# The last swiglu of a two-block diffusion transformer: products before the norm, operand parts side by side, all k tiles in one PSUM group

## The chip, the core and the metric

One core of a Trainium2 chip runs the whole kernel in one launch. The metric is the device time of that launch in microseconds: the median of several runs, and beside it one execution recorded by the hardware profiler, whose page and trace are read here. TensorE is called PE below, VectorE DVE, ScalarE ACT, GpSimd POOL and SyncE SP.

## What is computed

A block updates a latent sequence (256 tokens, 1024 features) and, where it is still read later, a context sequence of the same size: a gated swiglu, a mixer (short convolution in block 0, grouped attention in block 1) and a second gated swiglu. The part that the change rewrites is the end of block 1, for the 256 latent tokens alone: the output projection of the attention, the norm with its modulation, and the last swiglu.

```python
def _rms(t, g):
    y = t * lax.rsqrt(jnp.mean(t * t, axis=-1, keepdims=True) + NORM_EPS)
    return y * g

def _modulate(t, g, shift, scale):
    return _rms(t, g) * (1 + scale) + shift

def _swiglu(h, w13, w2):                       # w13: 1024 x 5632, w2: 2816 x 1024
    gte, up = jnp.split(h @ w13, 2, axis=-1)
    return (jax.nn.silu(gte) * up) @ w2

mod = (jax.nn.silu(c) @ mod_w[i] + mod_b[i])   # nine vectors of 1024 per block
...
lat = lat + mod[:, 1, 2] * (attention @ w_o)
lat = lat + 0.5 * mod[:, 2, 2] * _swiglu(
    _modulate(lat, norm_g[i, 2], mod[:, 2, 0], mod[:, 2, 1]), ffn_w13[i, 1], ffn_w2[i, 1])
```

Inputs, weights and result are 32-bit floats.

## The kernel before

**Layout.** Features lie on the 128 partitions, in `KT` = 8 tiles, and tokens on the free axis. The tile `x` holds 512 columns: latent tokens first (`S` = 256), then context (`T2` = 512 together). In the last part only the first 256 are computed.

**Products in three parts.** A product of two 32-bit operands is made from split operands. `split` (lines 97 to 99) writes `hi`, a rounded copy (ACT, line 98), and `lo`, the rest (DVE, line 99). `mm3` (lines 119 to 124) then issues three matmuls into one PSUM group: wh by mh, wh by ml, wl by mh. One call of `mm3` for one 128 x 128 weight tile is called a step. Weights come as raw tiles of up to 2048 columns over SP's queue (`load_raw`, tag `wr`, three buffers) and are split into halves of 1024 columns (`half`, tags `wh` and `wl`, four buffers each).

**The last swiglu.** `ffn(1, 1, hn, S, ...)` takes the hidden 2816 features as `NM` = 22 tiles, in `THIRDS` of 8, 7 and 7. For each tile `w13_mm` computes the gate half (`pg`) and the up half (`pu`), 8 k tiles each, 48 matmuls of 256 columns together; this is called a pair. `w13_post` applies silu (ACT), multiplies (DVE) and splits the product into `gh` and `gl`. After each third `project` multiplies the third's tiles by their part of w2, for 8 output tiles m (`py`), and `finish` adds the gated result to `x` (line 446, DVE). The last third's `finish` also sends each output tile from SP.

**The boundary before it.** The output projection is `project(by_pairs("wo"), ..., S, 0, 1)`. Its `tail_norm` squares each new tile of x and sums up over m (`square_add`, lines 220 to 228). After the last m, `rms_inv` sums over partitions on PE (line 237), takes the root (ACT), the reciprocal (DVE, line 246) and broadcasts the result with four small matmuls (line 248). `norm_k` then makes the normed, modulated operand parts `hh` and `hl` for each k (lines 256, 266 and 267), and the first pair's matmuls read them. `ready` (line 460) loads ACT's table for the root ahead of time.

**The modulation.** The nine vectors of each block are computed on DVE in 224 units (`mod_unit`, line 142, a product of 128 x 1024 with a row sum), from weight tiles that share the `wr` buffers and SP's queue with the others. They are spread over the kernel: `tick(n)` adds n to what is owed and issues that many whole units; `mod_ready` forces those that a vector still lacks when it is read. The argument `ev` of `ffn` and `project` is the number owed for each output tile m (1.7 in the second swiglu, 1.6 in the third). Four units belong to each 1 MB tile, but only two from vector 5 of block 1 on, where the context isn't needed any more.

**Order.** But for the opening, a scheduler of the framework lists the instructions of each engine ahead of time: among those that it reckons ready, the one written first. On the chip each engine goes through its list in order. PSUM is given out in eight banks, six of them (`psm`) for products, so three pairs can be open at once. `hot` hands out 1024 column tiles from a pool of 16, `gp` pairs of 512 column tiles, eight of each tag.

Of the kernel before, what the change touches and what calls it, by code (L numbers as in the profile page):

```python
# [9 lines left out]
F32 = mybir.dt.float32  # L10
F32R = mybir.dt.float32r
BF16 = mybir.dt.bfloat16
AF = mybir.ActivationFunctionType
ALU = mybir.AluOpType
AX = mybir.AxisListType

P = 128
D = 1024
KT = D // P
S = 256  # L20
T2 = 2 * S
NM = 22
# [19 lines left out]
def hybrid_kernel(ctx: ExitStack, tc: tile.TileContext, a: dict, out: bass.AP):  # L42
    nc = tc.nc
    const = ctx.enter_context(tc.tile_pool(name="const", bufs=1))
# [3 lines left out]
    gp = ctx.enter_context(tc.tile_pool(name="gp", bufs=8))  # L48
    tp = ctx.enter_context(tc.tile_pool(name="tp", bufs=2))
# [23 lines left out]
    x = act.tile([P, KT, T2], F32, name="x", tag="x")  # L73
# [140 lines left out]
    accs = {}  # L214
# [181 lines left out]
    def tail_norm(l, j, h):  # L396

        box = {}

        def tail(m, c0, c1):  # L400
            square_add(m, c0, c1)
            if m == KT - 1:
                if not box:
                    box["A"] = scale_of(l, j)
                    box["B"] = mod_ready(l, 3 * j)
                s = c0 // S

                def inv():
                    return rms_inv(s, (accs[s], accs[s, "last"]))

                def rest(part, ri):

                    if isinstance(h, Blocks):
                        h.block(s, part, box["A"], box["B"], ri, fine=s == 0 and part == 0)
                    else:
                        for k in range(4 * part, 4 * part + 4):
                            norm_k(s, k, h, box["A"], box["B"], ri)

                def both_parts():
                    ri = inv()  # L420
                    for part in range(2):
                        rest(part, ri)

                if s == 0:
                    keep = []

                    def one():
                        keep.append(inv())
                        rest(0, keep[0])

                    pending.append(one)
                    pending.append(lambda: rest(1, keep[0]))
                    if (l, j) == (1, 2):
                        flush()
                else:
                    flush()
                    pending.append(both_parts)

        return tail
# [268 lines left out]
    def lazy_gate(l, j):  # L708
        box = []

        def get():
            if not box:
                box.append(gate_of(l, j))
            return box[0]

        return get


    h = Plain()
# [11 lines left out]
    ris = []  # L731
    for s in range(2):
# [6 lines left out]
        out=sb1, in0=modb[:, 0, KT : 2 * KT], scalar1=1.0, scalar2=None, op0=ALU.add  # L739
# [81 lines left out]
    h = FirstBlocks(h, h32)  # L821
# [11 lines left out]
    hn = Plain()  # L833
    ffn(0, 0, h, T2, lazy_gate(0, 0), tail_norm(0, 1, hn), gs0)
    h = hn

    zs = []
    for m in range(KT):
# [16 lines left out]
        u = tp.tile([P, T2], F32, name=nm("u"), tag="gm", bufs=3)  # L855
# [21 lines left out]
    def by_pairs(key):  # L877
        box = {}

        def ws(m):  # L880
            if m // 2 not in box:
                box[m // 2] = load_w(a[key][m // 2])
            w = box[m // 2]
            return lambda k: w(k * 256 + (m % 2) * P)

        return ws

    hn = Blocks()
# [3 lines left out]
    )  # L892
    h = hn
    hn = Blocks()
    ffn(0, 1, h, T2, lazy_gate(0, 2), tail_norm(1, 0, hn), (), 1.7)
    h = hn


    hn = Plain()
    ffn(1, 0, h, T2, lazy_gate(1, 0), tail_norm(1, 1, hn), (), 1.6)  # L900
    h = hn
    ap = ctx.enter_context(tc.tile_pool(name="ap", bufs=2))

# [192 lines left out]
    for hd in range(HEADS):  # L1096
# [6 lines left out]
    mix(HEADS - 1, pts.pop(HEADS - 1))  # L1103


    hn = Plain(S)
    project(
        by_pairs("wo"), lambda k, c0, c1: aos[k], KT, lazy_gate(1, 1), tail_norm(1, 2, hn), S, 0, 1,
    )
    ffn(  # L1110
        1, 1, hn, S, lazy_gate(1, 2),
        lambda m, c0, c1: nc.sync.dma_start(out[m], x[:, m, :S]),
    )


def _layout(inp):
    f = lambda k: np.asarray(inp[k])
    d = {}

    def kp(w, width):  # L1120

        k, n = w.shape
        v = w.reshape(k // P, P, n // width, width).transpose(2, 1, 0, 3)
        return v.reshape(n // width, P, (k // P) * width)

    tok = np.concatenate([f("x")[0], f("ctx")[0]], axis=0)
    d["xT"] = tok.T.reshape(KT, P, T2).transpose(1, 0, 2)
    d["c2"] = np.stack([f("c")[0], f("c_ctx")], axis=0)
    d["ccol"] = d["c2"].reshape(2, KT, P).transpose(2, 1, 0)
    mw = f("mod_w")  # L1130
    m0 = mw[0][:, : 2 * D].reshape(KT, P, 2, 4, S)
    d["mod0"] = m0.transpose(2, 3, 1, 0, 4).reshape(2, 4, P, 2048)
    d["modT"] = mw.transpose(0, 2, 1).reshape(2, 36, 2, P, D).transpose(0, 1, 3, 2, 4).reshape(2, 36, P, 2048)
    d["modb"] = f("mod_b").reshape(2, 72, P).transpose(2, 0, 1)
    d["normg"] = f("norm_g").reshape(2, 3, KT, P).transpose(3, 0, 1, 2)
    w13 = f("ffn_w13").reshape(2, 2, KT, P, 2, NM, P)[:, :, :, :, ::-1]
    d["w13"] = w13.transpose(0, 1, 5, 3, 4, 2, 6).reshape(2, 2, NM, P, 2048)
    w2 = f("ffn_w2").reshape(2, 2, NM, P, KT // 2, 2, P)
    w2 = w2.transpose(0, 1, 4, 3, 5, 2, 6)
    n0, n1 = THIRDS[:2]  # L1140
    d["w2a"] = w2[:, :, :, :, :, :n0].reshape(2, 2, 4, P, 2 * n0 * P)
    d["w2b"] = np.stack(
        [
            w2[:, :, :, :, :, n0 + i * n1 : n0 + i * n1 + n1].reshape(2, 2, 4, P, 2 * n1 * P)
            for i in range(2)
        ],
        axis=2,
    )
    ci = f("conv_w_in")[0]
    cx = ci[:, D:].reshape(KT, P, 2, KT, P)  # L1150
    d["cw_cx"] = cx.transpose(3, 1, 0, 2, 4).reshape(KT, P, 2048)
    d["cw_b"] = kp(ci[:, :D], 256)
    d["cw_out"] = kp(f("conv_w_out")[0], 256)
    d["convk"] = f("conv_k")[0].reshape(3, KT, P).transpose(2, 0, 1)
    wqkv = f("attn_w_qkv")[0]
    d["wq"] = kp(wqkv[:, :D], 256)
    d["wk"] = kp(wqkv[:, D : D + 256], 256)[0]
    d["wv"] = kp(wqkv[:, D + 256 :], 256)[0]
    d["wo"] = kp(f("attn_w_o")[0], 256)
    d["qg"] = f("attn_q_g")[0].reshape(P, 1)  # L1160
    d["kg"] = f("attn_k_g")[0].reshape(P, 1)


    pos = np.arange(S)
    inv = np.float32(10000.0) ** (-np.arange(32, dtype=np.float32) / np.float32(32))
    ar = (pos // 64).astype(np.float32)[:, None] * inv
    ac = (pos % 64).astype(np.float32)[:, None] * inv
    ang = np.concatenate([ar, ar, ac, ac], axis=-1).astype(np.float32)
    d["cosT"] = np.cos(ang).T
    sign = np.where(np.arange(P) % 64 < 32, -1.0, 1.0).astype(np.float32)  # L1170
    d["sinT"] = np.sin(ang).T * sign[:, None]
    d["ident"] = np.eye(P, dtype=np.float32)
    d["rowsum"] = (np.arange(P)[:, None] % 32 == np.arange(2)).astype(np.float32)
    return {k: np.ascontiguousarray(v) for k, v in d.items()}
# [19 lines left out]
```

## Time and profile before

| | |
|---|---|
| median of 3 runs | 1596.06 us (1595.92 to 1598.62) |
| profiled execution, first to last instruction | 1599.4 us (the page gives no other time for it) |
| mean granted clock of PE | 0.993 |
| PE busy | 98% of the span, 10674 matmuls |
| DVE, ACT busy | 82%, 45% |
| output projection of the attention | about 1372 to 1396 us of the span |
| last swiglu | about 1403 to 1596 us |

The profiled execution is 3.3 us longer than the median run. In a profile, matmul records overlap (each starts before the one ahead of it has ended), so a busy share of PE is not a share of its peak; the time that a matmul costs is read from the distance of starts. L98 in a row is line 98 of the kernel. An arrow with a name (`<-DVE wl L99`) tells what an idle engine waited for. The granted clock is the share of full speed that PE was given.

### The profile page before, as it was taken

Reading aid. Unit: us, or ns where it says so; the run is one execution under the profiler, and the core shown is the slowest. Engines: PE = TensorE matmul, PEld = TensorE weight load, DVE = VectorE, ACT = ScalarE, POOL = GpSimd, SP = SyncE. Lnnn points to the kernel's source line nnn. Section 1 sums busy time; section 2 is a strip of 40 time slices with the busy share of each in tenths; the row PEclk is TensorE's granted clock in tenths of the full one; section 3 lists DMA queues with packets and bytes.
Section 4 is the critical chain, followed back from the end, with each engine's and each line's share of the span. In section 5 each row is a group of like instructions: output and inputs, shape, how many; then the busy total and the mean of one; then the engine's idle time right before and its main releaser. Section 6 shows DMA issues by size and latency. Waiting matters only on the chain.

```text
span 1599.4 us, 25805 instructions
## 1 busy us (share of the span) xinstructions
PE 1572.9 (98%) x10674; PEld 1452.2 (91%) x10674; DVE 1304.2 (82%) x1984; ACT 718.6 (45%) x1103; POOL 29.7 (2%) x20
## 2 busy tenths in 40 slices
PE   8999999999999999999999999999999998899999
PEld 6788998998888899999899899889899897899999
DVE  4778788879998879799798899898797799965554
ACT  5632452544322366335245375245254455554443
POOL 0000000000000000000000000000000005100000
PEclk9999999999999999999999999999999999989999
DMA  8455234234565422453443423452432554755462
GB/s 312 173 185 187 103 106 175 103 117 160 184 220 198 162 80 83 155 185 100 139 145 106 174 78 108 175 191 96 155 132 97 181 199 150 261 189 187 167 201 104
DMA packets 38422, 248.79 MB, mean 156 GB/s; under 512 B 5280, under 2 KB 7072, under 8 KB 12448
## 3 DMA queue, kind: packets, MB, share of 16 engines
q1 hardware_dynamic: 35712, 245.38, 44.0%
q10 hardware_dynamic: 2592, 1.76, 0.4%
q8 instruction: 83, 1.36, 0.3%
q14 instruction: 35, 0.29, 0.1%
HBM read 244.77 MB, written 1.05 MB: 154 GB/s over the span
## 4 chain that ended last, share of the span: by engine, by line
PE 87%; DVE 7%; DMA 3%; ACT 1%; issue 1%; POOL 0%; DVEq 0%; ACTq 0%; SPq 0%; POOLq 0%
PE py L122 8%; PE py L123 8%; PE py L124 8%; PE p L123 6%; PE p L122 6%; PE p L124 6%; PE q L124 5%; PE q L122 5%; PE q L123 5%; PE pg L122 3%; PE pg L123 3%; PE pg L124 3%; PE pu L124 3%; PE pu L123 3%; PE pu L122 3%; DVE junk L142 2%
## 5 line engine op out<-in xcount | busy, mean ns | idle before, releaser
L98 ACT ACTIVATE wh<-wr 128x1024 fp32r<-128x1024 f32 (+2 forms) x276 | 276.4, 1014 | 401.1 <-PE py L123 111.3
L99 DVE TENSOR_TENSOR wl<-wr,wh 128x1024 fp32r<-128x1024 f32 (+2 forms) x276 | 320.0, 1167 | 96.5 <-ACT wh L98 95.9
L142 DVE CUSTOM_DVE_ANT_0 junk<-wr,scbc,modb 128x1024 bf16<-128x1024 f32 x224 | 287.0, 1281 | 38.9 <-DMA wr<-in_modT 36.3
L122 PE MATMUL py<-gh,wh 128*128 128x512 f32 (+1 forms) x746 | 263.2, 353 | 0.0
L123 PE MATMUL py<-gl,wh 128*128 128x512 f32 (+1 forms) x746 | 263.1, 353 | 0.0
L124 PE MATMUL py<-gh,wl 128*128 128x512 f32 (+1 forms) x746 | 262.8, 352 | 0.0
L124 PEld LDWEIGHTS py<-gh,wl 128*128 128x128 f32 x746 | 141.1, 189 | 19.1
L122 PEld LDWEIGHTS py<-gh,wh 128*128 128x128 f32 x746 | 141.2, 189 | 18.5
L123 PEld LDWEIGHTS py<-gl,wh 128*128 128x128 f32 x746 | 141.2, 189 | 18.1
L99 DVE TENSOR_TENSOR wl<-ws,wh 128x1024 fp32r<-128x1024 f32 x108 | 131.8, 1224 | 29.1 <-ACT wh L98 28.9
L98 ACT ACTIVATE wh<-ws 128x1024 fp32r<-128x1024 f32 x108 | 113.5, 1058 | 68.0 <-PE p L123 35.5
L124 PE MATMUL p<-th,wl 128*128 128x256 f32 x432 | 122.2, 283 | 0.0
L123 PE MATMUL p<-tl,wh 128*128 128x256 f32 x432 | 122.2, 283 | 0.0
L122 PE MATMUL p<-th,wh 128*128 128x256 f32 x432 | 122.2, 283 | 0.0
L446 DVE SCALAR_TENSOR_TENSOR x<-py,G,x 128x256 f32<-128x256 f32 x168 | 74.1, 479 | 21.9 <-PE py L124 21.4
L122 PE MATMUL q<-bh,wh 128*128 128x256 f32 x320 | 90.6, 283 | 0.0
L123 PE MATMUL q<-bl,wh 128*128 128x256 f32 x320 | 90.6, 283 | 0.0
L124 PE MATMUL q<-bh,wl 128*128 128x256 f32 x320 | 90.6, 283 | 0.0
L122 PEld LDWEIGHTS p<-th,wh 128*128 128x128 f32 x432 | 82.9, 192 | 0.3
L123 PEld LDWEIGHTS p<-tl,wh 128*128 128x128 f32 x432 | 82.9, 192 | 0.3
L124 PEld LDWEIGHTS p<-th,wl 128*128 128x128 f32 x432 | 82.9, 192 | 0.0
L122 PE MATMUL pg<-hh,wh 128*128 128x256 f32 (+1 forms) x240 | 77.2, 322 | 3.7 <-ACT hh L266 3.6
(238 smaller groups left out, 4049.7 us busy)
## 6 DMA issues: line engine op xcount, KB each, us to landing
wr<-in_w SPq DMA_DIRECT2D x88, 1024.0 KB, 4.9
wr<-in_modT SPq DMA_DIRECT2D x64, 1024.0 KB, 4.9
wr<-in_w2b SPq DMA_DIRECT2D x32, 896.0 KB, 4.6
wr<-in_w2a SPq DMA_DIRECT2D x16, 1024.0 KB, 4.9
wr<-in_mod SPq DMA_DIRECT2D x8, 1024.0 KB, 6.7
wr<-in_cw_cx SPq DMA_DIRECT2D x8, 1024.0 KB, 5.0
wr<-in_cw_b SPq DMA_DIRECT2D x4, 1024.0 KB, 4.9
wr<-in_cw_out SPq DMA_DIRECT2D x4, 1024.0 KB, 4.9
```

The lines of the kernel that those rows point to most:

```text
L98: nc.scalar.activation(out=hi, in_=src, func=AF.Copy)
L99: nc.vector.tensor_tensor(out=lo, in0=src, in1=hi.bitcast(F32), op=ALU.subtract)
L122: nc.tensor.matmul(ps, wh, mh, start=first, stop=False, **kw)
L123: nc.tensor.matmul(ps, wh, ml, start=False, stop=False, **kw)
L124: nc.tensor.matmul(ps, wl, mh, start=False, stop=last, **kw)
L142: nc.vector.tensor_tensor_reduce(out=junk, in0=raw[:, j * D : j * D + D], in1=scbc[:, v, :], scale=1.0, scalar=modb[:, l, col : col + 1], ...
L446: nc.vector.scalar_tensor_tensor(out=x[:, m, s * S : s * S + S], in0=ps[:, o : o + S], scalar=g[:, m, s : s + 1], in1=x[:, m, s * S : s * ...
```

## The change

The output projection and the last swiglu are written out anew; `project` and `ffn` aren't called for them.

- After each output tile m of the projection, the operand parts `hi` and `lo` of x times scale (`A`) are made at once, without the norm, 256 columns and two more with the parts of the shift vector (`bs`). The first four pairs (`i < 4`) multiply these with `mm3`, 258 columns wide. 1/rms is computed within pair 1 and put in later: `first_post` multiplies both halves by it and adds the product of the shift columns (`shifts`), for gate in silu's bias and for up in the multiplication.
- Also in pair 1 the eight normed operands are made as before, but with `hi` and `lo` side by side in 512 columns (`ht`). From the fifth pair on `mm2` is used: wh by both parts in one matmul of 512 columns, then wl by `hi`, 256 columns, into the first half of the bank. `fold` adds the two halves (a copy on ACT, an addition on DVE).
- There are no thirds: all 22 pairs come first, their products `gs` are kept (16 in `gp`, six in `hot`), and then each m takes 22 k tiles in one PSUM group, with `mm2`. w2 comes in another layout, per two m as two tiles of 2048 columns and one of 1536.
- `ev` is 1.9 in the second and third swiglu instead of 1.7 and 1.6, and the modulation vectors that the norm reads are asked for ahead of the projection.

```diff
--- before.py
+++ after.py
@@ -892,12 +892,12 @@
     )
     h = hn
     hn = Blocks()
-    ffn(0, 1, h, T2, lazy_gate(0, 2), tail_norm(1, 0, hn), (), 1.7)
+    ffn(0, 1, h, T2, lazy_gate(0, 2), tail_norm(1, 0, hn), (), 1.9)
     h = hn
 
 
     hn = Plain()
-    ffn(1, 0, h, T2, lazy_gate(1, 0), tail_norm(1, 1, hn), (), 1.6)
+    ffn(1, 0, h, T2, lazy_gate(1, 0), tail_norm(1, 1, hn), (), 1.9)
     h = hn
     ap = ctx.enter_context(tc.tile_pool(name="ap", bufs=2))
 
@@ -1103,14 +1103,168 @@
     mix(HEADS - 1, pts.pop(HEADS - 1))
 
 
-    hn = Plain(S)
-    project(
-        by_pairs("wo"), lambda k, c0, c1: aos[k], KT, lazy_gate(1, 1), tail_norm(1, 2, hn), S, 0, 1,
-    )
-    ffn(
-        1, 1, hn, S, lazy_gate(1, 2),
-        lambda m, c0, c1: nc.sync.dma_start(out[m], x[:, m, :S]),
-    )
+    def mm2(ps, w, m, first, last):
+        nc.tensor.matmul(ps, w[0], m, start=first, stop=False, skip_group_check=True)
+        nc.tensor.matmul(
+            ps[:, :S], w[1], m[:, :S], start=False, stop=last, skip_group_check=True
+        )
+
+    def fold(ps):
+        t = tp.tile([P, S], F32, name=nm("fo"), tag="t", bufs=3)
+        nc.scalar.copy(t, ps[:, S:])
+        y = tp.tile([P, S], F32, name=nm("y"), tag="y", bufs=2)
+        nc.vector.tensor_tensor(out=y, in0=t, in1=ps[:, :S], op=ALU.add)
+        return y
+
+    def gated(m, y, g):
+        nc.vector.scalar_tensor_tensor(
+            out=x[:, m, :S], in0=y, scalar=g[:, m, :1], in1=x[:, m, :S],
+            op0=ALU.mult, op1=ALU.add,
+        )
+
+    W = S + 2
+    xat = [hot("xa") for _ in range(6)]
+
+    def xa(k, part):
+        i = 2 * k + part
+        o = (i % 3) * W
+        return xat[i // 3][:, o : o + W]
+
+    gate = gate_of(1, 1)
+    A = scale_of(1, 2)
+    B = mod_ready(1, 6)
+    bs = const.tile([P, 2, KT], F32R, name="bs", tag="bs")
+    split(bs[:, 0, :], bs[:, 1, :], B[:, :, 0])
+    wo = by_pairs("wo")
+    for m in range(KT):
+        if m == KT - 2:
+            ready()
+        w = wo(m)
+        ps = psum("py")
+        for k in range(KT):
+            mm3(ps[:, :S], w(k), aos[k], k == 0, k == KT - 1)
+        gated(m, ps[:, :S], gate)
+        square_add(m, 0, S)
+        hi, lo = xa(m, 0), xa(m, 1)
+        nc.scalar.activation(out=hi[:, :S], in_=x[:, m, :S], func=AF.Identity, scale=A[:, m, :1])
+        nc.vector.scalar_tensor_tensor(
+            out=lo[:, :S], in0=x[:, m, :S], scalar=A[:, m, :1], in1=hi[:, :S].bitcast(F32),
+            op0=ALU.mult, op1=ALU.subtract,
+        )
+        for part, t in enumerate((hi, lo)):
+            nc.scalar.copy(
+                t[:, S:], bs[:, part, m : m + 1].bitcast(F32).to_broadcast([P, 2])
+            )
+        tick(1)
+
+    gts = []
+
+    def g_tile(i):
+        if i < 16:
+            return gp.tile([P, T2], F32R, name=nm("g"), tag="gl" if i % 2 else "gh")
+        if i % 2 == 0:
+            gts.append(hot("gg"))
+        o = (i % 2) * T2
+        return gts[-1][:, o : o + T2]
+
+    def first_mm(pp, w, ks):
+        for k in ks:
+            for i in range(2):
+                mm3(
+                    pp[i][:, :W], w((1 - i) * 1024 + k * P), (xa(k, 0), xa(k, 1)),
+                    k == 0, k == KT - 1,
+                )
+
+    def shifts(pp):
+        c = tp.tile([P, 2], F32, name=nm("c"), tag="c", bufs=4)
+        for i in range(2):
+            nc.scalar.copy(c[:, i : i + 1], pp[i][:, S : S + 1])
+        return c
+
+    def product(g, sg, up, c=None):
+        gm = tp.tile([P, S], F32, name=nm("gm"), tag="gm", bufs=3)
+        if c is None:
+            nc.vector.tensor_tensor(out=gm, in0=sg, in1=up, op=ALU.mult)
+        else:
+            nc.vector.scalar_tensor_tensor(
+                out=gm, in0=up, scalar=c, in1=sg, op0=ALU.add, op1=ALU.mult
+            )
+        split(g[:, :S], g[:, S:], gm)
+
+    def first_post(pp, c, g, ri):
+        up = tp.tile([P, T2], F32, name=nm("up"), tag="sg", bufs=3)
+        for i in range(2):
+            nc.vector.tensor_tensor(
+                out=up[:, i * S : i * S + S], in0=pp[i][:, :S], in1=ri, op=ALU.mult
+            )
+        nc.scalar.activation(out=up[:, :S], in_=up[:, :S], func=AF.Silu, bias=c[:, :1])
+        product(g, up[:, :S], up[:, S:], c[:, 1:])
+
+    gs, held = [], []
+    ris = tp.tile([P, S], F32, name="rl", tag="ris0", bufs=1)
+    ht = []
+    for i in range(NM):
+        w = load_w(a["w13"][1, 1, i])
+        gs.append(g_tile(i))
+        pp = psum("pg"), psum("pu")
+        if i < 4:
+            first_mm(pp, w, range(4))
+            if i == 1:
+                pq = rms_inv(0, (accs[0], accs[0, "last"]))
+                nc.scalar.copy(ris, pq)
+            first_mm(pp, w, range(4, KT))
+            held.append((pp, shifts(pp), gs[-1]))
+            if i == 1:
+                for q in range(4):
+                    t = hot("h")
+                    ht.append(t)
+                    for k in (2 * q, 2 * q + 1):
+                        o = (k % 2) * T2
+                        hi, lo = t[:, o : o + S], t[:, o + S : o + T2]
+                        u = scaled(0, k, A, ris)
+                        b = B[:, k, :1]
+                        nc.scalar.activation(out=hi, in_=u, func=AF.Identity, bias=b)
+                        nc.vector.scalar_tensor_tensor(
+                            out=lo, in0=u, scalar=b, in1=hi.bitcast(F32),
+                            op0=ALU.add, op1=ALU.subtract,
+                        )
+            if i:
+                for one in held:
+                    first_post(*one, ris)
+                held = []
+        else:
+            for k in range(KT):
+                o = (k % 2) * T2
+                for j in range(2):
+                    mm2(
+                        pp[j], w((1 - j) * 1024 + k * P), ht[k // 2][:, o : o + T2],
+                        k == 0, k == KT - 1,
+                    )
+            y = fold(pp[0])
+            sg = tp.tile([P, S], F32, name=nm("sg"), tag="sg", bufs=3)
+            nc.scalar.activation(out=sg, in_=y, func=AF.Silu)
+            product(gs[-1], sg, fold(pp[1]))
+            tick(1)
+
+    gate = gate_of(1, 2)
+    box = {}
+
+    def w_last(m):
+        if m // 2 not in box:
+            t = m // 2
+            box[t] = (
+                load_w(a["w2l"][t, 0]), load_w(a["w2l"][t, 1]), load_w(a["w2m"][t], 12 * P)
+            )
+        o = m % 2
+        return lambda k: box[m // 2][o](k * P) if k < 16 else box[m // 2][2]((o * 6 + k - 16) * P)
+
+    for m in range(KT):
+        w = w_last(m)
+        ps = psum("py")
+        for k in range(NM):
+            mm2(ps, w(k), gs[k], k == 0, k == NM - 1)
+        gated(m, fold(ps), gate)
+        nc.sync.dma_start(out[m], x[:, m, :S])
 
 
 def _layout(inp):
@@ -1139,6 +1293,9 @@
...
+    wl = w2[1, 1].reshape(4, P, 2, NM, P)
+    d["w2l"] = wl[:, :, :, :16].transpose(0, 2, 1, 3, 4).reshape(4, 2, P, 2048)
+    d["w2m"] = wl[:, :, :, 16:].reshape(4, P, 12 * P)
...
```

## The prediction

> **What bounds the kernel now.** I read the page first, for the engine that sets the span:
>
> ```profile
> span 1599.4 us, 25805 instructions
> PE 1572.9 (98%) x10674; PEld 1452.2 (91%) x10674; DVE 1304.2 (82%) x1984; ACT 718.6 (45%) x1103; POOL 29.7 (2%) x20
> PE 87%; DVE 7%; DMA 3%; ACT 1%; issue 1%; POOL 0%; DVEq 0%; ACTq 0%; SPq 0%; POOLq 0%
> ```
>
> PE is busy for 98% and holds 87% of the chain that ended last. So the change pays only if it shortens what PE issues or closes a hole in PE. Then the table by stage, for the stretches that the diff rewrites (columns: stretch, length, busy of PE, PEld, DVE, ACT, POOL with counts, granted clock, DMA share, GB/s):
>
> ```profile
> 1372.00:1397.00 25.00, 23.28 (x189) 22.56 (x187) 23.37 (x40) 8.92 (x15) 0.00 (x0) 1.00 0.84 298
> 1397.00:1410.00 13.00, 9.57 (x47) 8.97 (x48) 12.75 (x28) 8.16 (x15) 0.00 (x0) 0.61 0.61 236
> 1410.00:1600.00 190.00, 186.12 (x1552) 185.92 (x1550) 100.49 (x133) 79.81 (x109) 0.00 (x0) 1.00 0.49 167
> ```
>
> Three different limits: the output projection (1372 to 1397) has VectorE full; the boundary to the last swiglu (1397 to 1410) has a granted clock of 0.61; the last swiglu itself has PE full and VectorE half idle. Each is costed from its own stretch.
>
> **The price of a step.** Matmul records overlap, so I take starts, not durations (timeline of PE, the last swiglu and a 512 wide run; columns start and duration):
>
> ```profile
> 1451.60 0.28 PE L122 MATMUL pu<-hh,wh 128*128 128x256 f32 x1
> 1451.72 0.28 PE L123 MATMUL pu<-hl,wh 128*128 128x256 f32 x1
> 1451.84 0.28 PE L124 MATMUL pu<-hh,wl 128*128 128x256 f32 x1
> 1451.96 0.28 PE L122 MATMUL py<-gh,wh 128*128 128x256 f32 x1
> ...
> 1140.00 0.39 PE L124 MATMUL py<-gh,wl 128*128 128x512 f32 x1
> 1140.22 0.39 PE L122 MATMUL py<-gh,wh 128*128 128x512 f32 x1
> 1140.45 0.39 PE L123 MATMUL py<-gl,wh 128*128 128x512 f32 x1
> 1140.68 0.39 PE L124 MATMUL py<-gh,wl 128*128 128x512 f32 x1
> ```
>
> 256 columns cost 0.120 us, 512 columns 0.68/3 = 0.227. So 256 further columns cost 0.107 and each instruction carries 0.013 beside its columns. mm3 is three of 256: 0.360. mm2 is one of 512 and one of 256: 0.347. The columns are the same 768; one instruction's 0.013 goes. Steps that become mm2: 18 tiles x 8 k x 2 = 288 in the first product, 8 m x 22 k = 176 in the second, 464 x 0.013 = 6.0 us. The first four pairs stay mm3 with two more columns: 4 x 16 x 3 x 2 x 0.107/256 = 0.16 us. **Term 1: -5.9.**
>
> A rule of the Trainium skill speaks against this term: the page "TensorE: Matmul & The Clock Gate", section "Back-to-back issue gap", has an isolated warm gap of N/2.4 + 2.5 ns. By it a step would go from 327.5 to 325.0 ns, and the term would be -1.2 less the 0.16. The rows above give 13 ns, not 2.5, for the fixed part.
>
> **The boundary.** PE from the last projection matmul on:
>
> ```profile
> 1396.04 0.28 PE L124 MATMUL py<-a,wl 128*128 128x256 f32 x1
> ...
> 1398.25 0.38 PE L237 MATMUL ss<-ones,sq 128*128 128x1 f32 x2 [0.46 <-ACT sq L220]
> ...
> 1400.53 1.22 PE L248 MATMUL ss<-ident,ri 128*128 128x128 f32 x4 [1.45 <-DVE ri L246]
> 1402.86 0.58 PE L122 MATMUL pg<-hh,wh 128*128 128x256 f32 x1 [1.11 <-ACT hh L266]
> ...
> 1405.16 0.41 PE L122 MATMUL pu<-hh,wh 128*128 128x256 f32 x1
> 1405.38 0.41 PE L123 MATMUL pu<-hl,wh 128*128 128x256 f32 x1
> ```
>
> From 1396.04 + 0.12 to 1402.86 no product runs: 6.7 us for sum of squares, 1/rms, broadcast and the first normed tile. After it the products start every 0.21 us: 8 pairs of 48 should take 46.1 us and take 1451.96 - 1402.86 = 49.1, so 3.0 us go to the lower clock. Together 9.7. After the change pair 0 multiplies x times scale, which exists for seven of eight k before the last projection matmul ends; the eighth needs x, hi and lo (about 2 us) and is wanted after 7 x 2 x 0.36 = 5.0. So PE runs on and the clock should hold. The eight statistics matmuls move into pair 1 and still cost PE about 0.9 (the four broadcasts 1.22 at the lower clock, so about half of that, and less for the four sums). **Term 2: -8.8** (end: -4, if pair 0's weights come 2 to 3 us late and the clock drops after all).
>
> **The projection.** Two waits for VectorE's split:
>
> ```profile
> 1383.46 0.28 PE L123 MATMUL py<-a,wh 128*128 128x256 f32 x1
> 1384.27 0.38 PE L124 MATMUL py<-a,wl 128*128 128x256 f32 x1 [0.53 <-DVE wl L99]
> ...
> 1390.00 0.28 PE L123 MATMUL py<-a,wh 128*128 128x256 f32 x1
> 1390.79 0.39 PE L124 MATMUL py<-a,wl 128*128 128x256 f32 x1 [0.50 <-DVE wl L99]
> ```
>
> They cost 0.69 + 0.67 and about 0.1 of restart each, 1.5. VectorE is full there because of the modulation products:
>
> ```profile
> L142 DVE CUSTOM_DVE_ANT_0 junk<-wr,scbc,modb 128x1024 bf16<-128x1024 f32 x8 | 10.2, 1279 | 1.0 <-DMA wr<-in_modT 1.0
> ```
>
> Counting ticks (22 x ev in each 512 wide swiglu, 4 + 16 in attention, and what gates force) 215 of 224 units are done when the projection begins; with 1.9 and 1.9 it is 222. In the row eight stand (the ninth falls behind 1397). So 7 units x 1.28 = 9.0 us leave VectorE here and 3.5 of their 1 MB loads leave SP's queue, ahead of the loads of wo. New here is lo, 8 operations of the kind that ends the kernel (0.48, last fence below), with hi and two small copies on ScalarE, which is busy 8.9 of 25. **Term 3: -1.2** (0 to -1.5).
>
> The seven units run earlier, four in the second swiglu and three net in the third. What covers them there:
>
> ```profile
> 659.00:703.00 44.00, 44.00 (x208) 36.91 (x207) 40.98 (x65) 10.22 (x12) 0.00 (x0) 1.00 0.51 175
> ...
> 1007.00:1053.00 46.00, 46.00 (x216) 38.55 (x215) 41.83 (x69) 8.05 (x10) 0.00 (x0) 1.00 0.52 188
> 1053.00:1125.00 72.00, 70.24 (x573) 69.29 (x572) 65.19 (x84) 40.36 (x63) 0.00 (x0) 1.00 0.39 133
> ...
> 1235.00:1278.00 43.00, 42.59 (x254) 37.78 (x252) 34.33 (x68) 17.40 (x26) 0.00 (x0) 1.00 0.47 168
> ```
>
> The second row's third holds 24 units, and PE idles 1.8 us behind it (third row); after the change it has 22 (fewer are forced by the gate), so some of that may go. The thirds of the first and last rows gain about 2 units each, 2.6 us of VectorE against 3.0 and 8.7 idle. Nothing excludes a delay at the end of the third swiglu, where SP also gets three more loads ahead of wq. **Term 4: +0.5** (-1.8 to +4).
>
> **VectorE in the first pairs.** Count from pair 0's first matmul. A pair is 48 x 0.12 = 5.8 us. The statistics stand behind half of pair 1, at 8.7; in the rows above sum to broadcast took 2.3 us, then 0.5 for the matmuls at full clock and 0.4 for the copy: 1/rms is there at 11.3 to 12. Then, written ahead of the epilogues, come the eight normed tiles; their present form on VectorE:
>
> ```profile
> 1401.79 1.26 DVE L256 SCALAR_TENSOR_TENSOR t<-x,A,ss 128x256 f32<-128x256 f32 x3 [0.19 <-PE ss L248]
> ...
> 1408.15 2.35 DVE L99 TENSOR_TENSOR wl<-wr,wh 128x1024 fp32r<-128x1024 f32 x2
> ```
>
> 6.4 us, in one block, with the next weight split queued behind it. So VectorE is at 17.7 to 18.4 before it multiplies pair 0 out of PSUM (2 x 0.4), perhaps with one split of 1.2 in between: 18.5 to 20.5. PSUM holds three pairs, so pair 3 waits for that; its turn is 3 x 5.8 + 0.9 = 18.3. Behind it queue two epilogues (3.3) and the split of pair 3's weights (2.4), while PE has the two thirds of pair 3 that need only wh. **Term 5: +2.5** (0, if the order interleaves, to 6.5, if everything named stands ahead).
>
> **Steady pairs and second product.** Durations of what each pair issues, from this stage (the copy from an earlier one):
>
> ```profile
> L98 ACT ACTIVATE wh<-wr 128x1024 fp32r<-128x1024 f32 x52 | 54.8, 1056 | 70.5 <-PE pg L123 46.0 <-PE py L123 17.7 <-issue 6.8
> L99 DVE TENSOR_TENSOR wl<-wr,wh 128x1024 fp32r<-128x1024 f32 x52 | 63.4, 1222 | 55.8 <-ACT wh L98 55.6
> L99 DVE TENSOR_TENSOR gl<-gm,gh 128x256 fp32r<-128x256 f32 x22 | 9.2, 419 | 0.0
> L530 DVE TENSOR_TENSOR gm<-sg,pu 128x256 f32<-128x256 f32 x22 | 9.1, 415 | 0.5 <-ACT sg L528 0.5
> L585 ACT COPY sg<-p 128x256 f32<-128x256 f32 x7 | 2.6, 367 | 2.2 <-PE p L124 2.2
> ```
>
> A fold is a copy like the last row and an add like gm's. VectorE per pair: 2 x 1.22 + 0.42 x 4 = 4.1 of 16 x 0.347 = 5.55. The tighter thing is the turn of a weight buffer, free at the pair's end and wanted a pair later: wh, wl, wl is 3.5 us in a row, with both folds (2 x 0.79) in between 5.1. It fits by a little; I take 0, to +4. In the second product m = 2t needs its last six k tiles in a buffer that its own first eight give back: free at 8 x 0.347 = 2.8, split by 2.8 + 1.06 + 1.22 + hand-offs = 5.2, wanted at 16 x 0.347 = 5.55: 0 again, and the ground of the slower rival below.
>
> **The end.**
>
> ```profile
> 1595.84 0.28 PE L124 MATMUL py<-gh,wl 128*128 128x256 f32 x1
> 1596.16 0.48 DVE L446 SCALAR_TENSOR_TENSOR x<-py,G,x 128x256 f32<-128x256 f32 x1 [2.03 <-PE py L124]
> ```
>
> Between these comes a fold, 0.37 + 0.42 and two hand-offs. **Term 6: +0.9.** The two thirds' boundaries inside the swiglu go, but no wait stands there now (1410 to 1600: PE busy 186.1 us, and its last matmul starts 185.8 in): 0.
>
> Sum: -5.9 - 8.8 - 1.2 + 0.5 + 2.5 + 0.9 = -12.0. Against the profiled execution: 1599.4 - 12.0 = 1587.4 of span. That span lies 3.3 us (0.2%) above the median of the runs, 1596.06; the terms are stretches on PE and carry over: **1584.0 us**.
>
> **Rivals.**
>
> Pile-up at pair 3 in full: term 5 at 6.5, and a hole that long drops the clock again as at 1402.86, 3 us more: 1584.0 + 4 + 3 = 1591. For it: program order puts the block first. Against: VectorE is idle from about 9 to 11. Chance 0.14.
>
> The boundary stays half open, because pair 0's weights are split late (their buffer is given back only when m = 5 ends, 5.8 us before they are wanted, and VectorE needs 2.4 of it): term 2 at -4, 1589. For it: VectorE is full there now. Against: term 3's 9 us. Chance 0.07.
>
> The step saves nothing, because 768 columns are 768 columns: without the fixed 0.013, term 1 is gone and the time is 1590. The two spacings above speak against it. Chance 0.02. (The page of the Trainium skill named above comes near this; with its 2.5 ns the time would be 1588.8.)
>
> Slower: the second product waits for its weights. Per two m it has six halves, and four buffers. Each half that PE must wait for costs its whole turn, 1.06 + 1.22 = 2.3 us; three of the six can be exposed, in four rounds: 12 x 2.3 = 27 us, 1611. It decides where a turn takes over 5.55 us, and turns the sign when six of the twelve are exposed. For it: the slack is 0.35 us. Against: ScalarE and VectorE have 110 and 90 us idle in the last swiglu now, and PE can be given the next m's products. Chance 0.10.
>
> **Numbers.** Forecast 0.67, rivals in their order 0.14, 0.07, 0.02, 0.10. The range runs from terms 3, 4 and 5 at their good ends together (1584.0 - 0.3 - 2.3 - 2.5 = 1579) to just past the pile-up (1592); outside are the slower rival and terms 4 and the steady pairs at their far ends. 0.2%, 3.2 us, is about what a measurement of this kernel tells from no change. Faster by more: 0.67 + 0.14 + 0.07 + 0.02, less 0.02 for a pile-up that meets term 4's far end, 0.88. Within: that 0.02 and 0.02 of the slower rival (five to seven halves exposed), 0.04. Slower: the rest of that rival, 0.08.
>
> **What would show it.** In the profile after: no hole and no lower clock between py of the projection and the first pg; 512 and 256 wide starts alternating at 0.227 and 0.120; two modulation units, not nine, after the projection begins; a wait of PE for a release by VectorE at the fourth pair, 0 to 6 us. Wrong would be: waits for wl inside py of the second product, or PE stretches ahead of the projection longer by over 4 us.

## The result and the profile after

The changed kernel takes 1587.12 us (median of 4 runs, 1585.96 to 1589.78) against 1597.34 before (4 runs, 1595.92 to 1599.79): ratio 0.9931, 95% interval [0.9913, 0.9948]. Forecast were 1584.0 against 1596.06, ratio 0.9924, with a range that ends at 1592. A second series of the same kernel gave 0.9943 [0.9922, 0.9963]. The page of the profiled execution:

```profile
span 1588.0 us, 25040 instructions
PE 1565.0 (99%) x10210; PEld 1423.9 (90%) x10210; DVE 1319.8 (83%) x2029; ACT 738.2 (46%) x1180; POOL 29.8 (2%) x20
PE 93%; DVE 3%; ACT 2%; DMA 1%; issue 1%; POOL 0%; DVEq 0%; POOLq 0%; ACTq 0%
```

464 matmuls fewer, as counted, and the chain is PE for 93% instead of 87%. By stage (stretch, length, busy of PE, PEld, DVE, ACT, POOL, granted clock, DMA share, GB/s):

```profile
1050.00:1118.00 68.00, 68.00 (x567) 67.92 (x566) 59.88 (x75) 38.42 (x61) 0.00 (x0) 1.00 0.34 122
1367.30:1390.50 23.20, 22.89 (x188) 22.69 (x189) 21.48 (x37) 16.69 (x38) 0.00 (x0) 1.00 0.82 297
1390.50:1409.50 19.00, 19.00 (x162) 18.95 (x160) 13.45 (x27) 11.83 (x25) 0.00 (x0) 1.00 0.38 137
1409.50:1419.00 9.50, 6.32 (x38) 6.03 (x38) 7.57 (x13) 3.77 (x9) 0.00 (x0) 0.82 0.34 118
1419.00:1588.00 169.00, 164.87 (x938) 142.98 (x937) 100.61 (x150) 85.88 (x142) 0.00 (x0) 1.00 0.48 168
```

The first row is the stretch behind the first third of the third swiglu: PE had idled 1.8 us there, now not at all. In the projection (second row) the two waits of before are gone, all but 0.2 us, with more on ScalarE. But the row begins behind a new wait, at the projection's start (rows of the changed kernel, and the last from the kernel before):

```profile
1364.98 1.28 DVE L142 CUSTOM_DVE_ANT_0 junk<-wr,scbc,modb 128x1024 bf16<-128x1024 f32 x1
1366.26 1.22 DVE L99 TENSOR_TENSOR wl<-wr,wh 128x1024 fp32r<-128x1024 f32 x1
1367.53 0.39 PE L124 MATMUL py<-a,wl 128*128 128x256 f32 x1 [1.43 <-DVE wl L99]
...
1372.22 0.39 PE L124 MATMUL py<-a,wl 128*128 128x256 f32 x1
```

A modulation unit now stands on VectorE ahead of the first split, and PE idles 1.4 us for the first `wl` (1.6 by the distance of starts); before, it waited less than 0.1. From its first to its last matmul the projection takes 26.3 us (1364.14 to 1390.40) against 25.9 before (1370.11 to 1396.04), so it gained nothing.

The boundary (third row) is closed: no hole, full clock. But the fourth row has a new hole, with a granted clock of 0.82. In PE's timeline:

```profile
1390.40 0.28 PE L124 MATMUL py<-a,wl 128*128 128x256 f32 x1
1390.52 0.28 PE L122 MATMUL pg<-xa,wh 128*128 128x258 f32 x1
...
1409.44 0.28 PE L123 MATMUL pu<-xa,wh 128*128 128x258 f32 x1
1412.90 0.50 PE L1107 MATMUL pg<-h,wh 128*128 128x512 f32 x1 [3.18 <-ACT wh L98]
1413.24 0.39 PE L1107 MATMUL pu<-h,wh 128*128 128x512 f32 x1
1413.47 0.30 PE L124 MATMUL pu<-xa,wl 128*128 128x258 f32 x1
...
1414.00 0.42 PE L124 MATMUL pu<-xa,wl 128*128 128x258 f32 x1
1414.21 0.42 PE L122 MATMUL pu<-xa,wh 128*128 128x258 f32 x1
```

After four matmuls of pair 3 PE's list has two of pair 4 (`h`), which wait 3.2 us for a weight half that ScalarE hasn't split; 44 matmuls of pair 3 stand behind them. Then starts are 0.21 us apart, as at the old boundary. What held ScalarE and VectorE, from their timelines:

```profile
1406.84 1.28 ACT L1200 ACT_TABLE_LOAD   x1
1410.14 1.05 ACT L98 ACTIVATE wh<-wr 128x1024 fp32r<-128x1024 f32 x1
1411.81 1.04 ACT L98 ACTIVATE wh<-wr 128x1024 fp32r<-128x1024 f32 x1
1411.88 1.22 DVE L99 TENSOR_TENSOR wl<-wr,wh 128x1024 fp32r<-128x1024 f32 x1
```

From 1401.7 to 1411.9 VectorE made the eight normed tiles and the first epilogues and split no weight at all. The first of these rows is ScalarE's load of a table, at the line of silu. The end of the kernel, with the fold between the last matmul and the gated sum:

```profile
1583.59 0.28 PE L1108 MATMUL py<-gg,wl 128*128 128x256 f32 x1
1583.91 0.37 ACT L1114 COPY fo<-py 128x256 f32<-128x256 f32 x1 [7.41 <-PE py L1108]
1584.31 0.42 DVE L1116 TENSOR_TENSOR y<-fo,py 128x256 f32<-128x256 f32 x1 [6.84 <-ACT fo L1114]
1584.77 0.48 DVE L1120 SCALAR_TENSOR_TENSOR x<-y,G,x 128x256 f32<-128x256 f32 x1
```

One caution for differences of 1 to 2 us: executions differ by several us in the kernel's opening, which no edit here touches. The run of 512 wide matmuls that begins at 60.2 us before begins at 57.8 in this profile; that is 2.4 of the 11.4 us between the two spans, and none of it is the change's. Small effects are therefore read from the traces at their place.

### The profile page after: what moved, and what is told of

Same layout as the page of the kernel before. It is cut to its first block, busy times and chain, and to the rows that moved or that the text cites. A ratio compares the mean times of both kernels' runs of the same rounds, so it can differ in the third digit from the quotient of the medians.

```text
span 1588.0 us, 25040 instructions
## 1 busy us (share of the span) xinstructions
PE 1565.0 (99%) x10210; PEld 1423.9 (90%) x10210; DVE 1319.8 (83%) x2029; ACT 738.2 (46%) x1180; POOL 29.8 (2%) x20
## 4 chain that ended last, share of the span: by engine, by line
PE 93%; DVE 3%; ACT 2%; DMA 1%; issue 1%; POOL 0%; DVEq 0%; POOLq 0%; ACTq 0%
PE py L122 9%; PE py L123 9%; PE py L124 9%; PE p L124 7%; PE p L123 7%; PE p L122 7%; PE q L122 5%; PE q L123 5%; PE q L124 5%; PE py L1107 3%; PE pg L1107 2%; PE pu L1107 2%; PE pg L122 2%; PE pg L123 1%; PE pg L124 1%; PE pu L124 1%
## 5 line engine op out<-in xcount | busy, mean ns | idle before, releaser
L123 PE MATMUL py<-gl,wh 128*128 128x512 f32 (+1 forms) x570 | 213.3, 374 | 0.0
L122 PE MATMUL py<-gh,wh 128*128 128x512 f32 (+1 forms) x570 | 213.3, 374 | 0.0
L124 PE MATMUL py<-gh,wl 128*128 128x512 f32 (+1 forms) x570 | 213.0, 374 | 0.0
L124 PEld LDWEIGHTS py<-gh,wl 128*128 128x128 f32 x570 | 107.3, 188 | 19.1
L122 PEld LDWEIGHTS py<-gh,wh 128*128 128x128 f32 x570 | 107.4, 188 | 18.5
L123 PEld LDWEIGHTS py<-gl,wh 128*128 128x128 f32 x570 | 107.4, 188 | 18.2
L446 DVE SCALAR_TENSOR_TENSOR x<-py,G,x 128x256 f32<-128x256 f32 x144 | 62.9, 477 | 6.3 <-PE py L124 6.0
L557 DVE TENSOR_TENSOR ws<-wr 128x1024 f32<-128x1024 f32 x54 | 65.7, 1218 | 0.0
```

The lines of the kernel that those rows point to most:

```text
L122: nc.tensor.matmul(ps, wh, mh, start=first, stop=False, **kw)
L123: nc.tensor.matmul(ps, wh, ml, start=False, stop=False, **kw)
L124: nc.tensor.matmul(ps, wl, mh, start=False, stop=last, **kw)
L446: nc.vector.scalar_tensor_tensor(out=x[:, m, s * S : s * S + S], in0=ps[:, o : o + S], scalar=g[:, m, s : s + 1], in1=x[:, m, s * S : s * ...
L557: tt(out=sm.rearrange("p (a b c) -> p a b c", a=2, b=2)[:, :, 0, :], in0=a21.unsqueeze(1).to_broadcast([P, 2, T2]), in1=self.raw[:, T2 : 3 ...
```

## The experiments

**The spreading of the modulation alone.** Two numbers changed in the kernel before:

```diff
-    ffn(0, 1, h, T2, lazy_gate(0, 2), tail_norm(1, 0, hn), (), 1.7)
+    ffn(0, 1, h, T2, lazy_gate(0, 2), tail_norm(1, 0, hn), (), 1.9)
-    ffn(1, 0, h, T2, lazy_gate(1, 0), tail_norm(1, 1, hn), (), 1.6)
+    ffn(1, 0, h, T2, lazy_gate(1, 0), tail_norm(1, 1, hn), (), 1.9)
```

> The kernel before with 1.9 and 1.9 in place of 1.7 and 1.6, nothing else. Theory (what the two profiles show): the stall behind the first third of the third swiglu (1.8 us of PE before, none after) and the two waits in the output projection (1.5 us) belong to the spreading of the modulation units; both go: 3 to 4 us less than before, PE idle behind that third under 0.3 us, two units after the projection begins. Rival: the rewritten projection removed its own waits, and the stall in the third swiglu differs from run to run: then 0 to 2 us less, and the waits for wl in the projection stay.

1592.3 us, ratio 0.9974 [0.9962, 0.9987], so about 4 us of the change come from these two numbers. By stage:

```profile
1050.00:1118.00 68.00, 68.00 (x568) 67.92 (x567) 59.84 (x75) 38.41 (x61) 0.00 (x0) 1.00 0.36 123
1365.60:1389.20 23.60, 22.73 (x190) 22.52 (x188) 20.11 (x34) 11.92 (x18) 0.00 (x0) 1.00 0.79 278
1389.20:1403.00 13.80, 10.32 (x64) 9.96 (x63) 9.36 (x20) 5.35 (x12) 0.00 (x0) 0.75 0.38 134
```

The stall in the third swiglu is gone without any new kernel text behind it, the projection is 0.5 us shorter, and even the old boundary is milder (a clock of 0.75 over 13.8 us instead of 0.61 over 13.0, and products begin 5.3 us after the projection's last instead of 6.7); VectorE no longer carries modulation there. The theory holds for the stall. In the projection the two waits went as well, but one of 0.9 us for the first `wl` stands at its start.

**The reverse.** The changed kernel with 1.7 and 1.6:

> The changed kernel with 1.7 and 1.6 as before. Theory (the spreading of the units gives its gain whatever the last stage is): the stall behind the first third of the third swiglu is back, 1.8 to 2.5 us, and more units stand before the projection, whose waits come back, 1 to 1.5 us: 3 to 4 us more than the changed kernel, 1590 to 1591. Rival (forced units ahead of the projection hurt more, since PE then waits for the scale vector): over 5 us more, 1593 or more.

1593.68 us, ratio 0.9965 [0.9953, 0.9977]: 3.5 to 5.4 us more than the changed kernel, by the ratios of its two series (0.9943 and 0.9931). The stall in the third swiglu is back (PE busy 68.36 of the 70.00 us from 1052 to 1122), one wait in the projection is longer than any before, and the boundary opens again:

```profile
1386.45 0.38 PE L124 MATMUL py<-a,wl 128*128 128x256 f32 x1 [1.97 <-DVE wl L99]
...
1399.35 0.38 PE L237 MATMUL ss<-ones,acc 128*128 128x1 f32 x2 [1.44 <-DVE acc L228]
1400.33 0.39 PE L122 MATMUL pg<-xa,wh 128*128 128x258 f32 x1 [0.60 <-ACT wh L98]
```

So the two numbers are more than an extra: without them VectorE is late at the boundary, and the unnormed start waits for its weights as the second rival of the prediction said. Counted from the stage behind the opening, this profile is 8.6 us behind the changed kernel's at the first gate matmul; 5.6 of them come back after it, as pair 3 has no hole of 3.3 us and the steps take 346.7 ns. The times don't decide between the 3 to 4 us that were expected and the rival's 5. The waits in these rows are for weight halves and for the sum of squares, not for the scale vector that the rival named.

**The norm first.** `if i < 4` becomes `if i < 0`, and the block that makes 1/rms and `ht` goes ahead of the loop:

> The changed kernel without the unnormed pairs: 1/rms and the eight normed operands are made ahead of pair 0, and all 22 pairs use mm2. Measures what the unnormed start is worth. From before's boundary: a hole of 6.7 us and 3.0 at the lower clock come back, the 3.3 + 1.9 of the changed kernel go, 64 more steps are mm2 (0.4 us): 4 us more than the changed kernel, 1590 to 1592; by theory H 353 per step. Rival: the start hides nothing that isn't given back, 1587.

1591.73 us, ratio 0.9960 [0.9945, 0.9975], against 1588.31 for the unaltered change on the same chip: 3.4 us more. The profile has the old boundary again:

```profile
1388.90:1395.70 6.80, 2.26 (x14) 1.80 (x12) 4.96 (x10) 3.84 (x9) 0.00 (x0) 0.70 0.63 235
1395.70:1403.00 7.30, 7.30 (x26) 6.26 (x27) 4.78 (x12) 2.36 (x6) 0.00 (x0) 0.58 0.02 8
```

6.8 us to the first product and a clock of 0.58 behind it. The unnormed start is worth about what was forecast, and gives more than half of it back at pair 3.

**The hole at pair 3, first remedy: spread the block.**

```diff
-            if i == 1:
-                for q in range(4):
+            if i:
+                for q in {1: (0,), 2: (1,), 3: (2, 3)}[i]:
```

> The changed kernel, but the eight normed operands are made two in pair 1, two in pair 2 and four in pair 3 instead of all in pair 1. Theory (VectorE's and ScalarE's queue holds up the weights of pairs 3 and 4): the 3.3 us hole of PE after the first four matmuls of pair 3 and the 1.9 us at the lower clock behind it go; 4 to 5 us less than the changed kernel, 1582 to 1583. Rival (the raw weights land late, or the list order of PE alone makes it): a hole of 2 us or more stays, 1586 to 1587.

1582.78 us, ratio 0.9901 [0.9883, 0.9919], 4.3 us less than the changed kernel. The stretch of the hole:

```profile
1411.00:1419.00 8.00, 7.86 (x57) 7.15 (x57) 8.00 (x17) 5.78 (x12) 0.00 (x0) 1.00 0.42 141
```

0.3 us of wait and the full clock. VectorE is busy for all of these 8 us. Its work in the whole kernel is the same (1319.1 us against 1319.8); only the order differs.

**Second remedy: the list of PE.** The block stays in pair 1; pair 3 issues its wh matmuls first:

```diff
+            if i == 3:
+                wh_first_mm(pp, w)     # all k: wh by hi, wh by lo; then all k: wl by hi
+            else:
+                first_mm(pp, w, range(4))
```

> The changed kernel, but pair 3 multiplies all its wh parts first and its wl parts last; nothing else. Before it, PE's list had two matmuls of pair 4 ahead of 44 of pair 3; here they come behind 37. Theory (half list order: PE stood still with 28 wh matmuls of pair 3 ready to run, 3.4 us of work): the hole shrinks to under 1.6 us and the clock holds, 3 to 5 us less than the changed kernel, 1582 to 1584; by theory H the pace is then 347 per step. Rival (everything waits for VectorE and ScalarE anyway): a hole of 3 us or more at another place, 1586 to 1588.

1583.13 us, ratio 0.9909 [0.9888, 0.9930]. PE around the place:

```profile
1415.05 0.28 PE L1186 MATMUL pu<-xa,wh 128*128 128x258 f32 x1
1415.41 1.22 PE L1188 MATMUL pu<-xa,wl 128*128 128x258 f32 x8
1416.48 0.39 PE L1107 MATMUL pg<-h,wh 128*128 128x512 f32 x1
1416.70 0.40 PE L1107 MATMUL pu<-h,wh 128*128 128x512 f32 x1
1416.94 1.22 PE L1188 MATMUL pg<-xa,wl 128*128 128x258 f32 x8
```

The split halves are as late as before, but PE works through what is ready, and the wait is 0.25 us. So the late weights alone didn't make the hole: it took two matmuls listed too early, with ready work behind them. The theory holds for the hole; its second half (347 per step where there is no hole) fell, the steps took 353.

**Both remedies:**

> Spread norm, and pair 3 with its wh parts first. The spread alone left a wait of 0.3 us in pair 3. Theory (both mend the same hole): no sum of the two gains, 1582 to 1584. Rival (each mends a part): 1579 to 1581. Its pace, in a list that again mixes pairs 4 and 5 at the start, shows whether such a mixed start goes with 353.

1582.22 us, ratio 0.9895 [0.9873, 0.9916]: they mend the same hole. All runs of this, and all of the spread alone in its first series, are faster than any of the changed kernel; between the two nothing can be told.

**The price of a step.** In the changed kernel the 176 steps of the second product start at (first and last wide matmul):

```profile
1521.52 0.40 PE L1107 MATMUL py<-g,wh 128*128 128x512 f32 x1
...
1583.35 0.40 PE L1107 MATMUL py<-gg,wh 128*128 128x512 f32 x1
```

61.83 us over 175 steps, 353.3 ns, where 347 were forecast. The first test makes three narrow matmuls of each step again, the second still into the other half of the bank:

```diff
-        nc.tensor.matmul(ps, w[0], m, start=first, ...)
+        nc.tensor.matmul(ps[:, :S], w[0], m[:, :S], start=first, ...)
+        nc.tensor.matmul(ps[:, S:], w[0], m[:, S:], start=False, ...)
```

> The changed kernel with each step of mm2 as three matmuls of 256 columns again, the second one still into the other half of the bank, with the same fold. Tells what the 353 ns of a measured step (347 were forecast) hang on. Theory W (a change of width from 512 to 256 costs 6 ns more): three starts 120 ns apart, 360 per step, 3.1 us more than the changed kernel. Theory B (going to and fro between two halves of a bank costs it): over 360, 366 or more, 6 us more.

1592.32 us in its one run, and a pair takes 5.76 us, 360.0 ns per step, throughout. The halves of the bank cost nothing, and the hole stays (3.3 us). Theory B falls. The second test groups the widths, sixteen and sixteen in a pair, eight, eight and six k tiles in the second product:

> The changed kernel, but mm2's matmuls grouped: in a pair all 16 of 512 columns and then all 16 of 256; in the second product eight, eight and six k tiles in the same way. Columns, instructions and sums are the same. Theory W (each change of width costs 6 ns): 227 + 120 = 347 per step, 2.9 us less than the changed kernel, 1584. Rival: a step costs 353 however it is ordered, 1587; or the wl parts, now wanted later, take a wait away elsewhere (the hole at the fifth pair), which the trace would show.

1587.36 us, ratio 0.9927 [0.9905, 0.9949], not to be told from the changed kernel, though the trace has 5.566 us per pair (347.9 per step) and 7.687 per m (349.4). From the end of the hole to the last matmul the profile takes 168.5 us against 170.7. Theory W gets most of what it asked for in the steps and nothing in the time that these runs can resolve. With the spread norm:

> Spread norm and grouped widths together. Theory H: the pace is 347 already with the spread norm, so grouping adds nothing: 1582 to 1583. Theory W (each change of width costs): steps below 346.7 or as low as forecast, and 0 to 2 us less than the spread norm alone.

1583.39 us, ratio 0.9911 [0.9895, 0.9928], 347.9 and 349.4 again. Here grouping is of no use, since the spread norm alone had the forecast pace:

```profile
1515.87 0.40 PE L1107 MATMUL py<-g,wh 128*128 128x512 f32 x1
...
1576.54 0.39 PE L1107 MATMUL py<-gg,wh 128*128 128x512 f32 x1
```

60.67 us for the same 175 steps, 346.7 ns, with the same instructions in the same order. Is that drawn by chance? Both programs were run again.

> The changed kernel again, unaltered. Its first profile has 353.3 ns per mm2 step throughout; the same stream behind the spread norm has 346.7 throughout. Theory H (how PE enters the stream decides: after the hole at the lower clock it falls into the slower pace): hole of 3.3 us and 353 again, 1586 to 1588. Rival R (the pace is drawn anew in each execution): any pace, not tied to the hole.

> The spread norm again, unaltered. Theory P (the pace of the mm2 stream is fixed by the program's list): 346.7 ns per step again, 1582 to 1584. Rival R (it is drawn anew in each execution): 350 to 353 can come, and then 1585 to 1586 in the profiled execution.

1588.31 and 1585.17 us (ratios 0.9943 [0.9922, 0.9963] and 0.9911 [0.9889, 0.9933]); the repeat of the spread (1582.54 to 1587.53) overlaps the changed kernel's runs. The profiles have 353.3 and 346.7 ns per step, as the first time; of the unprofiled executions the pace isn't known. In the changed kernel's repeat the hole came again, but not the lower clock:

```profile
1414.22 0.28 PE L123 MATMUL pu<-xa,wh 128*128 128x258 f32 x1
1417.67 0.50 PE L1107 MATMUL pg<-h,wh 128*128 128x512 f32 x1 [3.17 <-ACT wh L98]
...
1414.27:1423.77 9.50, 6.33 (x51) 6.04 (x51) 7.57 (x13) 4.32 (x10) 0.00 (x0) 1.00 0.35 123
```

The order of matmuls is the same to the last one and the wait is as long, yet the clock is 1.00 where it was 0.82, and the products behind the hole take 1.5 us less. So the slower pace doesn't need the lower clock, of which Theory H spoke. Both remedies together had 346.7, the change with its two numbers undone 346.7 (in spite of waits at the boundary), the norm first 353.3, the reordered pair 3 353.3. No rule by hole or clock fits these. The last run breaks the alternation at three places:

```diff
+            if i == 6:     # k = 2: wide, wide, narrow, narrow
+            if i == 10:    # k = 2: wide, narrow, narrow, wide
+            if i == 14:    # sixteen wide, then sixteen narrow
```

> The changed kernel with three breaks in the alternation of 512 and 256 columns: in pair 6 one place with two wide and two narrow matmuls in a row, in pair 10 one place with two narrow and two wide ones, in pair 14 all sixteen wide and then all sixteen narrow. The same matmuls otherwise. Theory L (the rhythm of starts is a state of PE that holds until something breaks it): 353.3 ns per step up to pair 6, and another pace, 346.7, behind one of the breaks, kept to the end. Rival F (the pace follows from the program's stream or from the hole, not from the rhythm): 353.3 again a pair behind each break.

1588.44 us in its one run, with the hole of 3.3 us. First matmuls of pairs 7, 9, 15 and 18:

```profile
1436.19 0.40 PE L1107 MATMUL pg<-h,wh 128*128 128x512 f32 x1
...
1447.29 0.40 PE L1107 MATMUL pg<-h,wh 128*128 128x512 f32 x1
...
1480.62 0.40 PE L1107 MATMUL pg<-h,wh 128*128 128x512 f32 x1
...
1497.58 0.40 PE L1107 MATMUL pg<-h,wh 128*128 128x512 f32 x1
```

32 steps in 11.10 us are 347; 48 steps in 16.96 are 353. This execution came out of the same hole with the lower price, kept it over the first two breaks, and took the higher one behind the third, to the end. That isn't the order that was expected, but it bears out Theory L's core: the pace is a state that a break in the order can change and that otherwise lasts. In the eight profiles whose alternation is unbroken it never changed once the alternation ran undisturbed. The change behind a break was seen once, in one execution. What sets the pace at the entry stays open; the same list up to pair 6 gave 353.3 twice and 346.7 here, so the list alone doesn't.

## Why the prediction was right, step by step

The time was inside the range, but the terms were not all right: the sum of -12.0 stands against -9.1 in the traces and -10.2 in the medians, and it comes that near because errors of up to 4 us offset each other. That much is luck. Measured in the traces, term by term:

| Term | forecast | measured |
|---|---|---|
| 1 steps | -5.9 | -3.2 (464 x 6.7 ns, and 0.1 in the first pairs) |
| 2 boundary | -8.8 | -8.3 (hole 6.7 and clock 3.0 gone, 1.4 of statistics kept) |
| 3 projection | -1.2 | +0.3 (waits of 1.5 became 0.2, and a new one of 1.6 at the start) |
| 4 units moved earlier | +0.5 | -3.6 (2.6 in the third swiglu, 1.0 between it and the projection) |
| 5 first pairs | +2.5 | +4.8 (hole 3.3, lower clock 1.5) |
| 6 end | +0.9 | +0.9 |
| sum | -12.0 | -9.1 |

With the 2.4 us of the opening this is the 11.4 between the spans but for 0.1. What the table hides: from the first gate matmul to the last matmul the changed kernel takes 193.07 us (1390.52 to 1583.59) and the kernel before 192.98. The steps and the old lower clock that are saved there go to the statistics, the hole and the new lower clock. The gain of this profile lies ahead of that, in the closed boundary and the modulation.

Terms 2 and 6 were read from rows of the right place and came out. In term 2 the steps held: the eighth operand was in time, the clock stayed, and the norm put first brought the hole and the lower clock back. Only the statistics were sized too low: from 1398.96 to 1401.84 PE starts twelve of their matmuls among twelve products, and these took 2.9 us where the products alone take 1.4.

Term 3's reason held and its gain didn't come. The modulation left the projection: the last unit starts at 1370.2, in the kernel before at 1397.7, and three units start behind its first matmul instead of nine. But the change asks for the norm's vectors ahead of the projection, and the prediction didn't ask what the first split of `wo` would queue behind. One unit of 1.28 us stood there, and PE's wait for it is as long as the two waits that went. Every profile of the changed kernel and of its variants has this wait, of 1.5 to 1.6 us.

Term 1 was mis-sized. The working took 0.227 and 0.120 from streams of one width and assumed that they hold in alternation. They do in some profiled executions (346.7) and not in others (353.3); both profiles of the changed kernel are of the second kind. The 0.16 for two more columns didn't come: the 48 matmuls of pair 0 start 118.5 ns apart on average. The Trainium skill's 2.5 ns of fixed part for the isolated gap ("TensorE: Matmul & The Clock Gate", section "Back-to-back issue gap") would have given an estimate of 1.2 us; no run agrees with it, as the three narrow matmuls differ from the step by 6.7 or 13.3 ns.

Term 4 had the wrong sign. The prediction saw that the worst third would hold two units fewer and allowed for -1.8, but then weighed the risk at the end of the third swiglu higher. In that third 21 units start before and 19 after. Its stall went as a whole, 2.6 us of PE time, and nothing came in its place: in the experiment with the two numbers alone it is 2.5. A further 1.0 us went between that swiglu and the projection; other profiles of the changed kernel have 0.5 to 1.1 there, the one with the two numbers alone 0.2, so the cause of that part isn't shown.

Term 5 was twice its size, and its mechanism half right. VectorE's block stood ahead of epilogues and splits as described, and the pile-up rival's lower clock came in this profile, though not in the repeat. But PE didn't wait for PSUM at pair 3's first matmul; it waited behind two matmuls of pair 4 that the scheduler had listed early. The prediction treated PE's order as the program's; it is a list made from reckoned times, and a short mistake in it cost 3.3 us, though the 28 wh matmuls that pair 3 had left stood ready behind them.

The slower rival didn't come: no wait for wl stands in the second product, whose 352 matmuls run without a hole from 1521.52 to 1583.59.

## What to carry to other kernels

When work is moved to close a hole, look at what the next weights must queue behind on the engines that prepare them, and at the order in which the busy engine's list takes its matmuls: here spreading one block of eight tiles over three pairs was worth 4 us, half of what closing the boundary had gained. Ask the same of side work that is moved ahead of a stage: one unit of 1.28 us in front of the projection's first split used up what its absence later had saved. A retimed stream of side work can be worth as much as a new data layout; test such a number by itself. Price an instruction in the mix in which it will run, since starts read from runs of equal instructions need not add up.

## What was not expected of the hardware

Alternating matmuls of 512 and 256 columns have two stable rhythms. In one, two steps repeat (starts 231, 112, 233 and 117 ns apart), 346.7 ns per step; in the other three (233, 117, 241, 120, 236, 113), 353.3. Each held for over 100 us in every profile with the alternation unbroken, and it changed once, behind a break in the order. Streams of 256 or of 512 columns alone kept their 120.0 and 227 ns.

A wait of PE of 3.3 us at pair 3 was followed by half the clock for about 3.4 us, some 4 us after its start (0.82 over 9.5 us), in four of the five profiles that have this wait. In the fifth, the repeat of the changed kernel, the clock stayed at 1.00. In the run with the numbers undone, waits of 1.4 and 0.6 us near each other were followed by starts 0.21 us apart (a clock of 0.50 from 1401.9 to 1405.2). The Trainium skill, "TensorE: Matmul & The Clock Gate", section "HAM oscillation — how this bites in real kernels", warns of idle gaps over about 3.4 us; here 3.3 were enough in four executions and not in a fifth, and what decides isn't shown.
